# A hybrid decoder layer on one core: narrower scores, the softmax's 1/sum moved into the head's norm, a chained product, and two gates computed as a pair

## The chip, the cores and the metric

The kernel runs on one core of one Trainium2 chip. The metric is the device time of one execution in microseconds (us). Before the change the median of three runs is 1358.22 us (1357.28 to 1360.21).

The engines are named as in the profile: PE (TensorE, matmuls, with PEld for its weight loads), DVE (VectorE), ACT (ScalarE), POOL (GpSimd), and SP, whose queue issues most DMAs. Each engine works through its instructions in a fixed order, which is decided when the program is built, and waits at an instruction until what it needs is there.

## The reference

One layer on x of 1024 tokens by 1024 channels, all in float32:

```python
xn = rmsnorm(x, norm_mix_w)
da_q, da_k, da_v, sw_q, sw_k, sw_v, g_da, g_sw = split_cols(xn @ w_in)   # 4352 columns
y_da = diff_attention(da_q, da_k, da_v, lam, 0.2, subln_w)
y_sw = sliding_window_attention(sw_q, sw_k, sw_v, sinks)
merged = sigmoid(g_da) * (y_da @ w_br_da) + sigmoid(g_sw) * (y_sw @ w_br_sw)
x = x + merged @ w_mix_out
x = x + conv_ffn(rmsnorm(x, norm_ffn_w), ...)     # up, causal conv of width 3, silu(gate) * val, down
return rmsnorm(x, norm_final_w)
```

The differential attention has 4 heads. For each head two score matrices (c = 0, 1) are made from 64 channels each; both are causal, carry a linear bias, and go through a softmax:

```python
p = softmax(logits)                       # over all keys up to the query
a = p[:, :, 0] - lam * p[:, :, 1]
o = a @ v                                 # 128 channels a head
o = rmsnorm(o, subln_w) * (1.0 - lam_init)
```

The window attention has 8 query heads in 2 groups, a window of 128 keys, and a sink logit for each head that enters only the softmax's sum.

## The kernel before

Everything is kept transposed: channels on the 128 partitions, the 1024 tokens along the free axis (two halves of 512). A float32 operand is split into a high part (rounded to fp32r by ACT) and a low part (the rest, by a DVE subtraction), and a product is three matmuls: high by high, high by low, low by high. A plain projection of 128 output channels costs 24 matmuls of 512 columns for each half of the tokens.

`project` (L251 on) computes 34 blocks of 128 channels of `w_in`. Five are plain. Eight pairs of blocks go through a Strassen-Winograd scheme: each pair's 2 x 2 problem (two output blocks, two token halves) takes seven products of 12 matmuls (`product`, names P1 to P7) where the plain way takes eight. For that POOL forms four sums of the weights (`sum_pair`, L87), ACT and DVE split them (`split_pair`), and DVE puts the products together (`recombine`). The last 13 blocks, which are gates, are not computed there: they are kept as filler, 26 halves of 24 matmuls, and `HALVES` says behind which attention step each is placed (`back_half`). A query or key block that comes out of a pair is scaled on POOL, split, and stored twice by SP; a gate block is stored as it is.

`attention` runs six units: four differential heads, then the two groups of the window attention, eight steps of 128 queries each. In `da_step` (step i, w = (i + 1) * 128 keys) PE writes the scores of each c into `sc` (two matmuls for each chunk of up to 512 columns; the width is rounded up to a multiple of 256), DVE adds the bias and finds the row minimum (L570), ACT takes the exponential with its row sum (L571), DVE forms the reciprocal of the sum (L572). ACT then scales the second matrix by -lam/sum (L577), DVE scales the first by its 1/sum and adds (L578). PE transposes the result, ACT and DVE split it, and `da_av` multiplies it with v. `da_norm` takes the norm of the head, over 128 channels, from sums of squares (`col_sums`, `rstd_cols`) and applies it in two pieces, one and two steps later (`later`). `sw_step` does the same for four heads at once: L653 to L661 the softmax, L663 four divisions by the sum on DVE, L670 transposes, L680 products, L687 the result, which is stored to DRAM and read back (`rest`, L705) to be split for the branch projections.

`down` (L968 on) multiplies the hidden activations (22 blocks) with `w_dn`. Blocks 0 to 5 are plain: 16 pieces (m, c), m the output block, c the first or second three blocks of input; the banks `pss[m, hf]` hold m's sum until DVE adds it to the residual in `x3` (L1034). Blocks 6 to 13 go through the seven products again: a loop over four output pairs (L1037 on) makes A11 B11 into a bank `y` that is kept, and A12 B21 into a bank `ps`, and adds both to `x3` (L1044); then come the other five. The first pair's weight sums are made early ("sums" in `ahead`): its two raw tiles lie in the ring `raw`, which has three buffers and through which every weight load goes. PSUM has four banks `d` and four `y`.

Of the kernel before, what the change touches and what calls it, by code (L numbers as in the profile page):

```python
# [31 lines left out]
LPAD, RPAD = 480, 480  # L32
LAM_INIT = 0.2

HALVES = ((2,), (0, 0, 0, 0, 1, 1, 0, 0), (0, 0, 0, 0, 1, 0, 1, 1), (0, 0, 0, 0, 1, 0, 1, 1), (0, 0, 0, 1, 1, 0, 1, 0),
          (1, 0, 1, 1, 0, 1, 0, 0), (1, 0, 1, 1, 0, 1, 1, 0), (4,))
NEGMASK = 1e30


# [4 lines left out]
class Trunk:  # L44
# [23 lines left out]
    def ahead(self, n):  # L68
        while len(self.wq) < n and self.wsrc and (self.wsrc[0][1] != "pair" or self.uw):
            src, nk, *eng = self.wsrc.pop(0)  # L70
            if nk == "sums":

                self.sums = self.split_pair(*self.sum_pair(src, True), 1, 3)
# [12 lines left out]

    def sum_pair(self, src, first=False):  # L87
# [5 lines left out]
        v = self.tl(self.wp, [P, 2, 4, P], "raw", bufs=RAW) if first else self.tl(self.uw, [P, 2, 4, P], "rv", bufs=2)  # L93
# [3 lines left out]
        tt(sa[:, 0], v[:, 0], v[:, 1], ALU.add)  # L97
# [120 lines left out]
    def plan(self):  # L218

        self.kind = {m: "q" if m < 4 or 12 <= m < 16 else "k" if m < 8 or m == 16 else "v" if m < 18 else "g" for m in range(34)}  # L220


        self.plain = [0, 4, 8, 18, 20]
        self.pairs = [(1, 5), (9, 2), (6, 10), (3, 7), (11, 12), (13, 16), (17, 14), (15, 19)]
        gates = list(range(21, 34))
        self.back = []
        todo = [(m, hf) for m in gates for hf in range(2)]
        for steps in HALVES:
            self.back.append([[todo.pop(0) for _ in range(n)] for n in steps])
# [11 lines left out]
        self.pieces = [(m, c) for m0 in (0, 4) for c in range(2) for m in range(m0, m0 + 4)]  # L241
# [182 lines left out]
    def attention(self):  # L424
        nc, tc = self.nc, self.tc
        with ExitStack() as ctx:
# [27 lines left out]
            for u in range(6):  # L454
                if st is None:
                    st = self.q_stacks(u), self.kv_stacks(u)
                if u < 4:
                    self.v_parts(u)
                elif u == 4:
                    self.sw_v(self.v32(17))  # L460
                y = self.tl(self.fpool, [P, T], "y", bufs=2) if u < 4 else None
                aT = None
                for i in range(NB):
                    if u < 4:
                        if i % 2 == 0:
# [12 lines left out]
                if u < 4:  # L478
                    later = self.da_norm(u, y)
# [73 lines left out]
    def da_step(self, h, i, st, aT):  # L553
# [1 line left out]
        q, k = st  # L555
        slope = 4.0 ** -(h + 1)
        w = (i + 1) * P
        wp = (w + 255) // 256 * 256
        pr, rr = [], []
        for c in range(2):  # L560
            sc = self.tl(self.psS, [P, T], "sc")
            qs = q[c][:, i * P:(i + 1) * P]
            for part in range(2):
                for n0 in range(0, wp, H2):
                    n1 = min(n0 + H2, wp)
                    nc.tensor.matmul(sc[:, n0:n1], qs, k[c][part][:, n0:n1], start=part == 0, stop=part == 1)  # L566
# [3 lines left out]
            nc.vector.tensor_tensor_reduce(L[:, :w], sc[:, :w], self.bias[:, o:o + w], slope, 3e38, ALU.add, ALU.min, s[:, 0:1])  # L570
            nc.scalar.activation(L[:, :w], L[:, :w], AF.Exp, bias=s[:, 0:1], scale=-1.0, accum_out=s[:, 1:2])  # L571
            nc.vector.reciprocal(s[:, 2:3], s[:, 1:2])  # L572
            if c == 1:
                nc.vector.tensor_tensor(s[:, 2:3], s[:, 2:3], self.neglam, ALU.mult)
            pr.append(L)
            rr.append(s[:, 2:3])
        nc.scalar.mul(pr[1][:, :w], pr[1][:, :w], rr[1])  # L577
        nc.vector.scalar_tensor_tensor(pr[0][:, :w], pr[0][:, :w], rr[0], pr[1][:, :w], ALU.mult, ALU.add)  # L578
        qo = (i % 2) * P
        for j0 in range(0, i + 1, 4):  # L580
            nj = min(4, i + 1 - j0)
# [19 lines left out]
    def da_norm(self, h, y):  # L601

        nc, ap = self.nc, self.ap
        sqs = []
# [7 lines left out]

        def sums():
            self.col_sums(ssq, sqs[1:], 4, 4)
            box.append(self.rstd_cols(ssq, 8, P))

        def half(hf):
            ps = self.tl(self.psT, [P, H2], "t")
# [20 lines left out]
    def sw_step(self, g, n, st):  # L639
# [18 lines left out]
        for h in range(4):  # L658
            nc.scalar.activation(L[:, h, :w], L[:, h, :w], AF.Exp, bias=s[:, 0, h:h + 1], scale=-1.0, accum_out=s[:, 2, h:h + 1])
        nc.vector.tensor_tensor(s[:, 2, :], s[:, 2, :], s[:, 1, :], ALU.add)  # L660
        nc.vector.reciprocal(s[:, 3, :], s[:, 2, :])  # L661
        for h in range(4):
            self.last = nc.vector.tensor_scalar(L[:, h, :w], L[:, h, :w], s[:, 3, h:h + 1], None, ALU.mult)  # L663
        po = self.tl(self.psT, [P, H2], "t")
        nblk = w // P
        parts = []
# [301 lines left out]
    def down(self):  # L968

        nc, tc = self.nc, self.tc  # L970
        with ExitStack() as ctx:
# [31 lines left out]
            for i, (m, c) in enumerate(self.pieces):  # L1003
# [5 lines left out]
                for hf in range(2):  # L1009
# [3 lines left out]
                    for q, j in enumerate(js):  # L1013
                        h, l = self.hs[hf, j]
                        for p, (v, x) in enumerate(((w[0], h), (w[0], l), (w[1], h))):
                            nc.tensor.matmul(pss[m, hf], v[:, q, :], x, start=c == q == p == 0, stop=c == 1 and q == n - 1 and p == 2)
                if i in (2, 8):
                    ms = slice(i // 8 * 4, i // 8 * 4 + 4)
# [10 lines left out]
                if i == len(self.pieces) - 1:  # L1029
                    sums.pop(0)()  # L1030
                if c == 1:
                    for hf in range(2):
                        x = col(m, hf)
                        tt(x, x, pss[m, hf], ALU.add)  # L1034
# [168 lines left out]
```

## Time and profile before

| | |
|---|---|
| median of three runs | 1358.22 us |
| profiled execution | 1359.85 us, of which the span of the trace is 1358.0 us |
| mean granted clock of PE | 0.997 |
| projections | from the start to about 219.8 us |
| attention, first score to last window product | 240.2 to 495.8 us |
| branch projections, first | 509.2 us |
| plain pieces of the down-projection | 1112.2 to 1177.5 us |

In the views, a row of instructions gives start and duration in us, engine, line, operation and operands. A row of a window gives its length, then for PE, PEld, DVE, ACT and POOL the busy time and in brackets the number of instructions, then PE's granted clock (1.00 is full), the share of the DMA engines that were busy, and GB/s. A row of waits gives who waited for whom, the total, how often, and the longest. Matmuls overlap: one that takes 0.39 us starts 0.23 us behind the one ahead of it.

### The profile page before, as it was taken

The page shows a single profiled execution, that of the slowest core. Times are in us where ns is not written, and L with a number is a line of the kernel's source. Part 1 is how long each engine was busy: PE and PEld are TensorE (multiplying, and loading weights), DVE is VectorE, ACT ScalarE, POOL GpSimd, SP SyncE. Part 2 cuts the span into 40 slices and gives each one's busy share as a digit, 9 for nine tenths or more (in the row PEclk, how much of TensorE's full clock was granted, in tenths as well). Part 3 has the DMA queues.
Part 4 walks back from the last instruction along what each step waited for, and adds up shares of the span by engine and source line. Part 5 has one row for each costly group of instructions (what it writes and reads, how often), then busy time and mean ns, then how long its engine had stood idle before and what let it go on. Part 6 is the DMA issues. An engine that isn't in the chain of part 4 may idle for free.

```text
span 1358.0 us, 17192 instructions
## 1 busy us (share of the span) xinstructions
PE 1337.9 (99%) x6316; PEld 1106.8 (82%) x6316; DVE 1009.0 (74%) x1485; ACT 623.3 (46%) x975; POOL 464.7 (34%) x326
## 2 busy tenths in 40 slices
PE   8999999999999999999999999999999999999997
PEld 6888888788888888888878888888888888788886
DVE  8746774688778966445689889888988898886454
ACT  9432232678776764344354333433343344333343
POOL 0436641000000015642455565556555611231011
PEclk9999999999999999999999999999999999999999
DMA  6334436755654246324522222222222248551342
GB/s 255 140 110 164 145 140 219 205 150 144 171 134 146 79 129 228 140 95 131 162 78 94 78 78 93 69 87 78 93 66 89 85 157 303 190 180 70 92 133 86
DMA packets 62757, 179.50 MB, mean 132 GB/s; under 512 B 6864, under 2 KB 15184, under 8 KB 62672
## 3 DMA queue, kind: packets, MB, share of 16 engines
q1 hardware_dynamic: 50640, 159.93, 36.5%
q10 hardware_dynamic: 12032, 18.46, 3.7%
q8 instruction: 50, 0.82, 0.3%
q14 instruction: 35, 0.29, 0.1%
HBM read 129.61 MB, written 48.76 MB: 131 GB/s over the span
## 4 chain that ended last, share of the span: by engine, by line
PE 61%; DVE 19%; issue 9%; POOL 5%; DMA 2%; ACT 2%; POOLq 0%; SPq 0%; DVEq 0%; ACTq 0%
POOL us L958 5%; PE g L151 5%; PE g L153 5%; PE g L152 5%; PE t L828 4%; PE t L830 4%; PE t L829 4%; PE y L989 3%; PE d L989 3%; PE sc L153 3%; PE sc L152 3%; PE sc L151 3%; DVE wl L113 3%; DVE c L951 3%; PE sc L566 3%
## 5 line engine op out<-in xcount | busy, mean ns | idle before, releaser
L963 ACT ACTIVATE c<-us,vecs 128x1024 f32<-128x1024 f32 x44 | 54.8, 1248 | 163.1 <-POOL us L958 159.6
L958 POOL TENSOR_TENSOR us<-us,rstd 128x1024 f32<-128x1024 f32 x42 | 100.3, 2407 | 53.9 <-DVE wl L132 35.6
L130 ACT CAST wh<-raw 128x1024 fp32r<-128x1024 f32 (+2 forms) x62 | 62.8, 1012 | 110.2 <-PE sc L152 34.9
L111 ACT CAST sh<-sf 128x1024 fp32r<-128x1024 f32 x60 | 62.8, 1050 | 101.3 <-POOL sf L98 62.4
L132 DVE TENSOR_TENSOR wl<-raw,wh 128x1024 fp32r<-128x1024 f32 (+2 forms) x62 | 84.7, 1366 | 31.8 <-ACT wh L130 31.2
L964 DVE SCALAR_TENSOR_TENSOR c<-us,vecs,c 128x1024 f32<-128x1024 f32 x44 | 66.3, 1509 | 51.2 <-ACT c L963 51.2
L97 POOL TENSOR_TENSOR sf<-rv 128x512 f32<-128x512 f32 x29 | 41.9, 1446 | 162.0 <-DMA rv<-in_w_up 63.5
L113 DVE TENSOR_TENSOR sl<-sf,sh 128x1024 fp32r<-128x1024 f32 x60 | 83.7, 1397 | 8.0 <-ACT sh L111 8.0
L718 POOL TENSOR_TENSOR gr<-gr,rstd 128x1024 f32<-128x1024 f32 x16 | 40.3, 2521 | 130.3 <-PE t L670 91.1
L151 PE MATMUL g<-xh,wh 128*128 128x512 f32 x208 | 83.5, 402 | 0.3 <-ACT g L496 0.3
L152 PE MATMUL g<-xl,wh 128*128 128x512 f32 x208 | 83.1, 400 | 0.0
L153 PE MATMUL g<-xh,wl 128*128 128x512 f32 x208 | 82.8, 398 | 0.0
L168 POOL TENSOR_TENSOR rs<-ms,mhalf 128x8 f32<-128x8 f32 (+2 forms) x9 | 14.5, 1609 | 169.6 <-DVE ms L166 163.6
L570 DVE CUSTOM_DVE_ANT_0 L<-sc,bias 128x128 f32<-128x128 f32 (+7 forms) x64 | 47.9, 752 | 22.4 <-PE sc L566 17.3
L99 POOL TENSOR_TENSOR sf<-raw,rv 128x512 f32<-128x512 f32 x29 | 40.4, 1391 | 58.7 <-DVE sl L113 58.7
L965 DVE SCALAR_TENSOR_TENSOR c<-us,vecs,c 128x1024 f32<-128x1024 f32 x44 | 57.2, 1301 | 0.6
L98 POOL TENSOR_TENSOR sf<-sf,raw 128x512 f32<-128x512 f32 x30 | 56.7, 1890 | 1.6
L550 POOL MEMSET aT<- 128x128 f32 x32 | 6.1, 206 | 145.5 <-PE t L597 99.6
L113 DVE TENSOR_TENSOR wl<-raw,wh 128x1024 fp32r<-128x1024 f32 (+1 forms) x34 | 52.5, 1545 | 0.1
L566 PE MATMUL sc<-u,u 128*128 128x512 f32 (+1 forms) x192 | 51.1, 371 | 1.4 <-issue 0.8
L571 ACT ACTIVATE L<-L,sm 128x128 f32<-128x128 f32 (+7 forms) x64 | 49.4, 776 | 6.3 <-DVE sm L570 5.3
L151 PE MATMUL sc<-mh,wh 128*128 128x512 f32 x128 | 49.8, 389 | 0.0
(437 smaller groups left out, 4317.6 us busy)
## 6 DMA issues: line engine op xcount, KB each, us to landing
u<-qd SPq DMA_DIRECT2D x72, 256.0 KB, 6.6
raw<-in_w_down SPq DMA_DIRECT2D x28, 512.0 KB, 3.7
raw<-in_w_in SPq DMA_DIRECT2D x26, 512.0 KB, 4.2
hr<-hd SPq DMA_DIRECT2D x50, 256.0 KB, 5.3
raw<-in_w_up SPq DMA_DIRECT2D x23, 512.0 KB, 3.5
hd<-c SPq DMA_DIRECT2D x22, 512.0 KB, 2.7
rv<-in_w_up SPq DMA_DIRECT2D x21, 512.0 KB, 3.5
gr<-gd SPq DMA_DIRECT2D x16, 512.0 KB, 3.4
```

Source lines behind the costliest of these rows:

```text
L111: nc.scalar.copy(hi, src)
L113: nc.vector.tensor_tensor(lo, src, hi.bitcast(F32), ALU.subtract)
L130: self.hi = nc.scalar.copy(wh, raw)
L132: self.lo = (eng or nc.vector).tensor_tensor(wl, raw, wh.bitcast(F32), ALU.subtract)
L151: nc.tensor.matmul(ps, wh[:, kc + o, :], ah, start=first and n == 0, stop=False)
L152: nc.tensor.matmul(ps, wh[:, kc + o, :], al, start=False, stop=False)
L153: nc.tensor.matmul(ps, wl[:, kc + o, :], ah, start=False, stop=last and n == len(kcs) - 1)
L566: nc.tensor.matmul(sc[:, n0:n1], qs, k[c][part][:, n0:n1], start=part == 0, stop=part == 1)
L958: i = (nc.vector if m % NF == 0 else nc.gpsimd).tensor_tensor(us[:, 2:], us[:, 2:], self.rstd, ALU.mult)
L964: nc.vector.scalar_tensor_tensor(c, us[:, 1:T + 1], cw[1], c, ALU.mult, ALU.add)
L965: nc.vector.scalar_tensor_tensor(c, us[:, 0:T], cw[0], c, ALU.mult, ALU.add)
L989: nc.tensor.matmul(ps, v[:, n, :], x, start=n == i == 0, stop=n == len(js) - 1 and i == 2)
```

## The change

Six things are changed together.

1. `HALVES`, `pairs`: gates 21 and 22 become a ninth pair in the projections; 22 filler halves remain, placed anew.
2. `da_step`: the scores are computed for w columns only (i = 0 keeps 256). For w = 640 they are placed 128 columns into the tile, so that the chunks are 384 and 256 wide.
3. `da_step`, `da_norm`: the exponentials are no longer scaled by 1/sum. With s0 and s1 the two sums, the combination is p0 + p1 * (-lam * s0 / s1), which is s0 times the old one; s0 is kept for each query in a tile of the head, and the norm takes it out: the mean of squares is multiplied by 1/s0 squared, and the resulting factor by 1/s0, on POOL.
4. `sw_step`: the division of the fourth head goes from DVE to POOL; what the gates' first use waits for (`self.last`) becomes the reciprocal.
5. `down`: output blocks 4 to 7 come first in the pieces. For blocks 0 to 3 the first half's bank is not added to `x3` behind the pieces: A12 B21 is accumulated into it, and the sum is added once.
6. `sum_pair`: the second raw tile of the early sums lies in an `sl` buffer and not in the ring `raw`.

```diff
+        lo = P if w == 640 else 0
+        cuts = ((0, 256),) if i == 0 else ((0, w),) if w <= H2 else ((0, H2 - lo), (H2 - lo, w))
...
-                for n0 in range(0, wp, H2):
-                    n1 = min(n0 + H2, wp)
-                    nc.tensor.matmul(sc[:, n0:n1], qs, k[c][part][:, n0:n1], start=part == 0, stop=part == 1)
+                for n0, n1 in cuts:
+                    nc.tensor.matmul(sc[:, lo + n0:lo + n1], qs, k[c][part][:, n0:n1], start=part == 0, stop=part == 1)
...
-            nc.scalar.activation(L[:, :w], L[:, :w], AF.Exp, bias=s[:, 0:1], scale=-1.0, accum_out=s[:, 1:2])
-            nc.vector.reciprocal(s[:, 2:3], s[:, 1:2])
-            if c == 1:
-                nc.vector.tensor_tensor(s[:, 2:3], s[:, 2:3], self.neglam, ALU.mult)
+            nc.scalar.activation(L[:, :w], L[:, :w], AF.Exp, bias=s[:, 0:1], scale=-1.0, accum_out=s[:, 1:2] if c else self.s0[:, i:i + 1])
             pr.append(L)
-        nc.scalar.mul(pr[1][:, :w], pr[1][:, :w], rr[1])
-        nc.vector.scalar_tensor_tensor(pr[0][:, :w], pr[0][:, :w], rr[0], pr[1][:, :w], ALU.mult, ALU.add)
+        nc.vector.reciprocal(s[:, 2:3], s[:, 1:2])
+        nc.vector.tensor_scalar(s[:, 3:4], self.s0[:, i:i + 1], s[:, 2:3], self.neglam, ALU.mult, ALU.mult)
+        nc.vector.scalar_tensor_tensor(pr[0][:, :w], pr[1][:, :w], s[:, 3:4], pr[0][:, :w], ALU.mult, ALU.add)
...
-            box.append(self.rstd_cols(ssq, 8, P))
+            nc.vector.reciprocal(r0, s0)
+            nc.vector.tensor_tensor(t, r0, r0, ALU.mult)
+            nc.vector.tensor_tensor(t, t, ssq[:, :NB], ALU.mult)
+            rs = self.rstd_cols(t, 8, P)
+            nc.gpsimd.tensor_tensor(rs, rs, r0, ALU.mult)
...
-        nc.vector.reciprocal(s[:, 3, :], s[:, 2, :])
+        self.last = nc.vector.reciprocal(s[:, 3, :], s[:, 2, :])
         for h in range(4):
-            self.last = nc.vector.tensor_scalar(L[:, h, :w], L[:, h, :w], s[:, 3, h:h + 1], None, ALU.mult)
+            eng = nc.gpsimd if h in (3,) else nc.vector
+            eng.tensor_scalar(L[:, h, :w], L[:, h, :w], s[:, 3, h:h + 1], None, ALU.mult)
...
-        self.pairs = [(1, 5), (9, 2), (6, 10), (3, 7), (11, 12), (13, 16), (17, 14), (15, 19)]
-        gates = list(range(21, 34))
+        self.pairs = [(1, 5), (9, 2), (6, 10), (3, 7), (11, 12), (13, 16), (17, 14), (15, 19), (21, 22)]
+        gates = list(range(23, 34))
...
-                    for hf in range(2):
+                    for hf in range(m < 4, 2):
                         x = col(m, hf)
                         tt(x, x, pss[m, hf], ALU.add)
...
-                y, ps = bank(1), bank(0)
+                y, ps = bank(1), pss[m, 0]
...
-                self.product(ps, (wh[:, 4:8], wl[:, 4:8]), "B21")
+                self.product(ps, (wh[:, 4:8], wl[:, 4:8]), "B21", first=False)
```

`HALVES` (the lists are the units; the first entry stands ahead of them, the last behind them):

```diff
-HALVES = ((2,), (0, 0, 0, 0, 1, 1, 0, 0), (0, 0, 0, 0, 1, 0, 1, 1), (0, 0, 0, 0, 1, 0, 1, 1), (0, 0, 0, 1, 1, 0, 1, 0),
-          (1, 0, 1, 1, 0, 1, 0, 0), (1, 0, 1, 1, 0, 1, 1, 0), (4,))
+HALVES = ((2,), (0, 0, 0, 0, 1, 1, 0, 0), (0, 0, 0, 0, 1, 0, 0, 1), (0, 0, 0, 0, 1, 0, 1, 0), (0, 0, 0, 1, 1, 0, 1, 0), (1, 0, 0, 1, 0, 1, 1, 0), (1, 0, 1, 1, 0, 0, 1, 0), (3,))
```

More of the change, by code (lines that the diff above doesn't have):

```diff
@@ L71, in ahead @@
             if nk == "sums":
-                self.sums = self.split_pair(*self.sum_pair(src, True), 1, 3)
+                self.sums = self.split_pair(*self.sum_pair(src, True, "sl"), 1, 3)
             elif nk == "rest":
@@ L85, in ahead, with sum_pair @@
             self.wsrc[0] = src, nk, None, None, self.load_raw(src, nk)
-    def sum_pair(self, src, first=False):
+    def sum_pair(self, src, first=False, idle=None):
         nc = self.nc
@@ L92, in sum_pair @@
         nc.sync.dma_start(g.rearrange("p a k c -> p (a k) c"), src[0])
-        v = self.tl(self.wp, [P, 2, 4, P], "raw", bufs=RAW) if first else self.tl(self.uw, [P, 2, 4, P], "rv", bufs=2)
+        v = self.tl(self.wp, [P, 2, 4, P], "raw", bufs=RAW) if first and not idle else self.tl(self.uw, [P, 2, 4, P], idle or "rv", bufs=2)
         nc.sync.dma_start(v.rearrange("p a k c -> p (a k) c"), src[1])
@@ L240, in plan @@
         n, n2 = N1 // 2, NF - N1 - 8
-        self.pieces = [(m, c) for m0 in (0, 4) for c in range(2) for m in range(m0, m0 + 4)]
+        self.pieces = [(m, c) for m0 in (4, 0) for c in range(2) for m in range(m0, m0 + 4)]
         src += [(self.w_dn[m:m + 2, :, n * c:n * c + n, :].rearrange("m p k c -> p m k c"), 2 * n) for m, c in self.pieces[::2]]
@@ L464, in attention @@
                     if u < 4:
+                        if i == 0:
+                            self.s0 = self.tl(self.st, [P, NB], 's0', bufs=2)
                         if i % 2 == 0:
@@ L557, in da_step @@
         w = (i + 1) * P
-        wp = (w + 255) // 256 * 256
-        pr, rr = [], []
+        lo = P if w == 640 else 0
+        cuts = ((0, 256),) if i == 0 else ((0, w),) if w <= H2 else ((0, H2 - lo), (H2 - lo, w))
+        pr = []
         for c in range(2):
@@ L569, in da_step @@
             o = 896 - i * P
[L570 to L574 removed]
+            nc.vector.tensor_tensor_reduce(L[:, :w], sc[:, lo:lo + w], self.bias[:, o:o + w], slope, 3e38, ALU.add, ALU.min, s[:, 0:1])
+            nc.scalar.activation(L[:, :w], L[:, :w], AF.Exp, bias=s[:, 0:1], scale=-1.0, accum_out=s[:, 1:2] if c else self.s0[:, i:i + 1])
             pr.append(L)
[L576 to L578 removed]
+        nc.vector.reciprocal(s[:, 2:3], s[:, 1:2])
+        nc.vector.tensor_scalar(s[:, 3:4], self.s0[:, i:i + 1], s[:, 2:3], self.neglam, ALU.mult, ALU.mult)
+        nc.vector.scalar_tensor_tensor(pr[0][:, :w], pr[1][:, :w], s[:, 3:4], pr[0][:, :w], ALU.mult, ALU.add)
         qo = (i % 2) * P
@@ L603, in da_norm @@
         nc, ap = self.nc, self.ap
-        sqs = []
+        sqs, s0 = [], self.s0
         for hf in range(2):
@@ L614, in sums @@
             self.col_sums(ssq, sqs[1:], 4, 4)
-            box.append(self.rstd_cols(ssq, 8, P))
+            r0, t = (self.tl(self.st, [P, NB], n, bufs=2) for n in ("r0", "r2"))
+            nc.vector.reciprocal(r0, s0)
[3 more added lines that the diff above has]
+            nc.gpsimd.tensor_tensor(rs, rs, r0, ALU.mult)
+            box.append(rs)
         def half(hf):
@@ L1015, in down @@
                         for p, (v, x) in enumerate(((w[0], h), (w[0], l), (w[1], h))):
-                            nc.tensor.matmul(pss[m, hf], v[:, q, :], x, start=c == q == p == 0, stop=c == 1 and q == n - 1 and p == 2)
+                            nc.tensor.matmul(pss[m, hf], v[:, q, :], x, start=c == q == p == 0, stop=c == 1 and q == n - 1 and p == 2 and (m > 3 or hf > 0))
                 if i in (2, 8):
-                    ms = slice(i // 8 * 4, i // 8 * 4 + 4)
+                    ms = slice(4 - i // 8 * 4, 8 - i // 8 * 4)
                     nc.sync.dma_start(x3[:, ms], self.x2d[ms].rearrange("m p t -> p m t"))
```

## The prediction

> **What bounds the kernel now.** I read the page's busy times first, then PE's waits, then the timelines of the places that the change touches.
>
> ```profile
> PE 1337.9 (99%) x6316; PEld 1106.8 (82%) x6316; DVE 1009.0 (74%) x1485; ACT 623.3 (46%) x975; POOL 464.7 (34%) x326
> PE t L277 <- ACT wh L130: 6.6, 1, 6.6
> PE y L828 <- ACT wh L130: 1.1, 1, 1.1
> PE sc L566 <- issue: 0.8, 1, 0.8
> PE y L830 <- DVE wl L132: 0.6, 1, 0.6
> PE sc L566 <- DMA u<-qd: 0.6, 1, 0.6
> 219.77 0.39 PE L151 MATMUL g<-xh,wh 128*128 128x512 f32 x1
> 230.42 0.39 PE L153 MATMUL g<-xh,wl 128*128 128x512 f32 x1
> 309.40 0.28 PE L596 MATMUL t<-aT,v 128*128 128x256 f32 x1
> 311.43 0.28 PE L598 MATMUL t<-aT,v 128*128 128x256 f32 x1
> ```
>
> TensorE is the bound: 99% busy, and behind the 6.6 us of the first load its waits are a few tenths each. So time falls with matmuls that go, by the distance between two starts, not by the 0.39 us of one, since they overlap. From 219.77 to 230.42 lie the 48 matmuls of two gate halves: 10.65 / 47 = 0.2266 us for 512 columns. From 309.40 to 311.43 lie 18 of 256 columns: 2.03 / 17 = 0.119 us. What else can change is a wait, and the largest behind the start is this one:
>
> ```profile
> 1182.72 0.39 PE L830 MATMUL d<-h,wl 128*128 128x512 f32 x1
> 1184.23 0.50 PE L828 MATMUL y<-h,wh 128*128 128x512 f32 x1 [1.12 <-ACT wh L130]
> 1184.56 0.40 PE L829 MATMUL y<-h,wh 128*128 128x512 f32 x1
> 1185.57 0.50 PE L830 MATMUL y<-h,wl 128*128 128x512 f32 x1 [0.61 <-DVE wl L132]
> 1186.75 0.63 PE L828 MATMUL y<-h,wh 128*128 128x512 f32 x1
> 1187.18 0.63 PE L829 MATMUL y<-h,wh 128*128 128x512 f32 x1
> 1180.00:1200.00 20.00, 18.27 (x73) 14.33 (x72) 18.91 (x30) 8.90 (x14) 0.00 (x0) 0.91 0.65 215
> ```
>
> The second A12/A11 weight of the down-projection comes late: starts 1182.72 and 1184.23 are 1.51 apart instead of 0.23, 1184.56 and 1185.57 1.01, so 2.1 us are lost. Then the spacing is 0.43 instead of 0.23 for some eight matmuls, with the granted clock of the slice at 0.91: about 1.7 us more, 3.8 in all. [...]
>
> **The change, part by part.**
>
> *Ninth pair.* Gates 21 and 22 cost 4 halves of 24 matmuls; as a pair they cost 7 products of 12. 96 - 84 = 12 matmuls of 0.2266: **-2.7 us**. The pair adds POOL sums, splits and recombinations in the projections, where DVE has room beside PE:
>
> ```profile
> 180.00:200.00 20.00, 20.00 (x90) 16.57 (x89) 15.70 (x14) 6.42 (x8) 9.69 (x5) 1.00 0.34 132
> 271.50:306.60 35.10, 35.07 (x222) 30.27 (x222) 28.33 (x82) 27.51 (x62) 3.21 (x9) 1.00 0.56 157
> 402.25:495.80 93.55, 93.09 (x512) 76.96 (x511) 78.50 (x288) 64.20 (x188) 2.46 (x2) 1.00 0.34 109
> ```
>
> The first row is a pair: PE full, DVE 15.7 of 20. A ninth one of the same kind hides there. Its loads replace the two gates' loads; its two stores of `us` stand on SP where the last pair's three stood, ahead of the bias and the q/k stacks.
>
> ```profile
> 223.39 0.32 SPq L421 DMA_DIRECT2D qd<-us  x1
> 223.76 0.46 SPq L384 DMA_DIRECT2D gd<-us  x1
> 226.21 2.43 SPq L507 DMA_DIRECT2D u<-qd  x4
> ```
>
> Today the stacks follow at 226.21, 2.5 us behind the gate's store, which is ready at 223.76, itself held behind the key/query store at 223.39 (that one goes through POOL and ACT first). Two plain gate stores are ready about 1.5 us sooner, while by the order of the two programs 75 filler matmuls instead of 82 stand ahead of the first score (1.6 us less cover). This about cancels; the 0.8 us "issue" wait at that place may go: **-0.5** (-0.8 to +1.5).
>
> *Scores of used columns.* For i = 2, 4, 6 one chunk of 512 columns becomes 384: 3 steps x 2 c x 2 parts x 4 heads = 48 matmuls; no row shows 384 columns. Bounds: nothing saved (0), or as cheap as 256 (48 x 0.107 = 5.2). Between 0.119 and 0.2266 the middle is 0.173, since the spacing follows the columns at both ends: 48 x 0.054 = **-2.6**.
>
> *Sum in the norm.* Per step the ACT scaling and one reciprocal go; `tensor_tensor` on one column becomes `tensor_scalar`. Rows of the heads:
>
> ```profile
> L577 ACT ACTIVATE L<-L,sm 128x128 f32<-128x128 f32 (+7 forms) x32 | 24.3, 775 | 2.7 <-DVE sm L574 2.3 <-DVE sm L572 0.3
> L572 DVE RECIPROCAL sm<-sm 128x1 f32<-128x1 f32 x64 | 9.6, 157 | 6.2 <-ACT L L571 6.0
> ```
>
> ACT loses 24.3 us, DVE 32 x 0.157 = 5.0, and each chain from score to transpose is 0.8 us shorter. None of it is PE's time: worth 0 on its own; it is what pays for the lost filler. The norm gains a reciprocal, two products and one POOL product per head (about 0.16 each on DVE); its results are asked for a step later.
>
> *Lost filler.* In the attention PE has 4 of 26 gate halves (21.8 us) and 2.6 us of scores less to put over the DVE chains. A head (271.5 to 306.6) has DVE 28.3 of 35.1; it loses 1.3 us of DVE (8 x 0.157) and, by the order of the two programs, 1 to 4 us of PE, and stays between 80 and 86%. The window's part (402.25 to 495.80) is tighter: DVE 78.5, PE full in 93.6. In the program of the changed kernel 184 gate matmuls instead of 220 stand between the first and the last of its steps: 36 x 0.2266 = 8.2 us less, leaving 85.4 for DVE's 78.5 less one weight split (1.2) and the moved divisions:
>
> ```profile
> L663 DVE TENSOR_SCALAR L<-L,sw 128x256 f32<-128x256 f32 (+1 forms) x60 | 17.4, 344 | 0.3
> L653 DVE CUSTOM_DVE_ANT_0 L<-sc,bias 128x256 f32<-128x256 f32 (+1 forms) x52 | 19.8, 406 | 2.7 <-PE sc L650 2.7
> 198.98 2.41 POOL L386 TENSOR_TENSOR us<-us,rstd 128x1024 f32<-128x1024 f32 x1 [9.15 <-DVE us L402]
> 199.07 3.40 DVE L113 TENSOR_TENSOR sl<-sf,sh 128x1024 fp32r<-128x1024 f32 x1 [0.17 <-ACT sh L111]
> 1212.39 1.30 POOL L97 TENSOR_TENSOR c<-raw 128x512 f32<-128x512 f32 x1 [4.81 <-DVE sl L113]
> ```
>
> 60 divisions take 17.4, so 16 of them 4.6: DVE 72.7 of 85.4, 85% against 84% today. Stalls of PE grow little. Bounds: 0, and DVE's 72.7 with the 15.1 us of gaps that it has today (93.6 - 78.5), which is 87.8, 2.4 beyond 85.4, and as much again in the four heads: +5. Since a gap of DVE shrinks when its chain is asked for sooner, I take **+1.4**.
>
> *One of 4 divisions on GpSimd.* No row shows a POOL division. Bounds: 0.29 (DVE's pace) and 1.30 (POOL's sum of 512 columns, two inputs); I take half of that row, 0.65, less than the 0.9 that DVE's other three take beside it. POOL has 2.5 us of work in the window's 93.6. But a POOL operation can hold DVE: the split at 199.07 took 3.40 us, the whole 2.41 of POOL's operation longer than its usual 1.2. In a step, DVE's long operations read PSUM, and only the 4-column ones have two SBUF inputs, so I count 0 beyond the +1.4. [...]
>
> *End of attention.* The last window step's result is stored, read back and split; today
>
> ```profile
> 495.01 1.19 PE L680 MATMUL t<-aT,v 128*128 128x512 f32 x4
> 504.32 3.73 SPq L705 DMA_DIRECT2D yr<-yd  x4
> 512.91 2.36 DVE L749 TENSOR_TENSOR yl<-yr,yh 128x1024 fp32r<-128x1024 f32 x2 [0.21 <-ACT yh L748]
> ```
>
> 58 filler matmuls (13.1 us) and 24 of the first branch (5.4) cover it from 495.9 on, to 514.5; the last split ends at 515.3, used a little later. After the change 37 remain (8.4), but four of the next output's stand ahead and the halves interleave, so that the last part is used 18.8 us behind the last product instead of 20.5. Splits follow their loads, which wait for four buffers: **+0.4** (0 to +3).
>
> *Down-projection.* The chain into the first product's bank removes 4 of the 16 adds ahead of the stall, and holds `d` banks that nobody else needs. The `sl` buffer frees one of three raw buffers. The late weight is number two; ACT and DVE ahead of it:
>
> ```profile
> 1182.61 0.62 ACT L748 CAST h<-hr 128x512 fp32r<-128x512 f32 x1 [0.52 <-DVE hr L937]
> 1183.13 1.04 ACT L130 CAST wh<-raw 128x1024 fp32r<-128x1024 f32 x1
> 1176.56 1.21 DVE L132 TENSOR_TENSOR wl<-raw,wh 128x1024 fp32r<-128x1024 f32 x1
> 1183.70 0.68 DVE L1034 TENSOR_TENSOR x<-x,y 128x512 f32<-128x512 f32 x1
> 1184.30 1.21 DVE L132 TENSOR_TENSOR wl<-raw,wh 128x1024 fp32r<-128x1024 f32 x1
> ```
>
> Raw data is there; ACT's cast waits behind a cast that waits for DVE, and DVE has 11 operations of 0.6 between the first weight's split (1176.56) and the second's (1184.30). Four adds gone are 2.4 us. But the new order puts other splits into their place (12 operations between the two), and `sl` is loaded only when PE is done with the parts that lay there (eleven or twelve pieces in, about 1161), so POOL's sums and their splits move from about 1159 to 1165 and closer to the stall. Bounds: -3.8 (it goes) and +2 (as long again). I take **-1.5**, less than half of it. 3.8 - 1.5 = 2.3 would stay.
>
> **Sum**, against the profiled execution (span 1358.0, time 1359.85): -2.7 - 0.5 - 2.6 + 1.4 + 0.4 - 1.5 = -5.5, 1354.3. The median of the runs is 1358.22, 1.6 below the profiled one, so **1352.7 us**.
>
> **Rivals.** *The stall goes altogether and attention hides all:* -2.7 - 2.6 - 0.5 - 3.8 = -9.6, **1348.6**. For it: four adds fewer ahead of a 2.1 us delay; against: the order above. *The gain comes back as waits of PE in the attention*, +5 instead of +1.4: **1356.5**, no change. For it: DVE at 85% with chains; against: the window's steps run at 84% now with 0.5 us of PE idle. *Slower: GpSimd's quarter is late.* Place: the transposes of head 3 in each of 16 steps. If it takes 1.3 us and its start waits for DVE, a step's chain is 0.4 to 0.8 us longer and DVE is held 0.65; it decides from 85.4 us on, when a step exceeds 5.3 us of PE: 72.7 + 16 x 1.3 = 93.5, 8 us over. With half-clock stretches behind some gaps (1.7 each, two or three), 1352.7 + 8 + 4 = **1365**. For it: the row at 199.07; against: POOL is empty there.
>
> **How the numbers follow.** Forecast 60%, stall gone 16%, gain lost 12%, slower 12%. A measurement tells 0.2% (2.7 us) from nothing. Faster by that means below 1355.5: nearly all of the forecast (its own range 1350 to 1356) and the first rival, 74%; within 1355.5 to 1360.9: 14%; slower: 12%. The range 1348.5 to 1360 takes in the forecast and the first two rivals, and leaves the slower one out.
>
> **What would show it.** 6304 matmuls or so; 48 scores of 384 columns at 0.17 apart; the attention some 24 us shorter, projections 19 longer; PE's wait for `wh`/`wl` near 1180 between 0 and 2 us and the clock there 0.91 or 1.00; POOL divisions near 0.65. Wrong would make it: PE gaps over 1 us in the window's steps, DVE operations stretched beside POOL's divisions, or 384 columns paced like 512.

## The result, and the profile after

The changed kernel takes 1365.8 us (median of 6 runs, 1364.41 to 1366.56) against 1358.4 for the kernel before on the same chip: ratio 1.0054, 95% interval 1.0043 to 1.0066. It is slower by 7.4 us; 1352.7 was forecast, and the range ended at 1360. The span of its profiled execution is 1364.3 us.

The page of the changed kernel, busy times and granted clock by slices:

```profile
PE 1345.2 (99%) x6304; PEld 1104.3 (81%) x6304; DVE 1015.9 (74%) x1454; ACT 603.9 (44%) x942; POOL 485.5 (36%) x350
...
PEclk9999999999999999999999999999999999999999
```

The largest waits of PE (the 6.7 us of the first load left out; who waited for whom, total, how often, longest), and two windows, the steps of the window attention and the place of the old stall:

```profile
PE d L173 <- POOL rs L167: 1.0, 1, 1.0
PE d L158 <- ACT sl L1086: 0.8, 1, 0.8
PE sc L151 <- DVE yl L756: 0.7, 3, 0.3
PE g L150 <- DVE gr L741: 0.5, 1, 0.5
PE y L837 <- DVE wl L131: 0.5, 1, 0.5
PE t L687 <- DVE aT L681: 0.5, 2, 0.2
```

```profile
400.00:500.00 100.00, 98.18 (x552) 79.17 (x551) 85.80 (x315) 70.25 (x207) 17.56 (x18) 1.00 0.35 106
1180.00:1200.00 20.00, 19.53 (x86) 15.85 (x86) 19.68 (x29) 7.64 (x11) 0.00 (x0) 1.00 0.75 246
```

What was forecast of the work came: 6304 matmuls, 12 fewer; ACT 19.4 us less; and at 1180 the stall is down to one wait of 0.5 us, with 86 matmuls started in the slice instead of 73 and the clock at 1.00. The waits are small, too small for 7.4 us and the gain that was forecast besides; the two largest were there before, with 1.0 and 0.8 us. And PE is busy 7.3 us *more* than before (1337.9), with fewer matmuls at the same clock. So their starts must lie further apart. That shows where there is no wait. In the mix (384 matmuls of 512 columns), the first and the last before, then the first, the 49th and the last after:

```profile
596.22 0.39 PE L151 MATMUL sc<-mh,wh 128*128 128x512 f32 x1
683.03 0.39 PE L153 MATMUL sc<-mh,wl 128*128 128x512 f32 x1
```

```profile
598.58 0.40 PE L150 MATMUL sc<-mh,wh 128*128 128x512 f32 x1
610.33 0.39 PE L150 MATMUL sc<-mh,wh 128*128 128x512 f32 x1
687.00 0.39 PE L152 MATMUL sc<-mh,wl 128*128 128x512 f32 x1
```

Before, 86.81 / 383 = 0.2267 us from start to start. After, the first 48 hold two gaps: starts at 603.14 and 609.07 follow just behind the ends of DVE's operations on `ml`, at 603.09 and 609.01. From the 49th on there is none: 76.67 / 335 = 0.2289. In three products of the hidden layer (36 matmuls of the T operands with the sums of weights, `sh` and `sl`), before and after:

```profile
788.89 0.39 PE L828 MATMUL t<-T_0h,sh 128*128 128x512 f32 x1
796.82 0.39 PE L830 MATMUL t<-T_3h,sl 128*128 128x512 f32 x1
```

```profile
794.34 0.40 PE L835 MATMUL t<-T_0h,sh 128*128 128x512 f32 x1
802.47 0.39 PE L837 MATMUL t<-T_3h,sl 128*128 128x512 f32 x1
```

7.93 / 35 = 0.2266 became 8.13 / 35 = 0.2323. The diff touches neither stage. What the two stages share with it is memory: `s0`, `r0` and `r2` are new tiles of 32 bytes a partition, two buffers each, 192 bytes in the pool `st`, which lies ahead of the weights on the left side of SBUF. In the built programs the first raw weight tile lies at byte 9216 of a partition before, and at 9408 after; all later tiles of the left side move with it (`wh`, `wl`, the inputs of the branches and most of the hidden layer's). The right side (`xh`, `xl`, `mh`, `ml`, and in the hidden layer `sh`, `sl`) starts at the other end: `xh` is at 163328 in both programs. Before, the tiles of the large products all start at multiples of 512; after, left and right are 192 bytes out of step.

### The profile page after: what moved, and what is told of

The parts are those of the page before. It is cut to its first block, busy times and chain, and to the rows that moved or that the text cites. A ratio compares the mean times of both kernels' runs of the same rounds, so it can differ in the third digit from the quotient of the medians.

```text
span 1364.3 us, 17160 instructions
## 1 busy us (share of the span) xinstructions
PE 1345.2 (99%) x6304; PEld 1104.3 (81%) x6304; DVE 1015.9 (74%) x1454; ACT 603.9 (44%) x942; POOL 485.5 (36%) x350
## 4 chain that ended last, share of the span: by engine, by line
PE 86%; DVE 5%; POOL 3%; DMA 3%; issue 1%; ACT 1%; POOLq 0%; SPq 0%; ACTq 0%; DVEq 0%
PE t L837 14%; PE t L836 14%; PE t L835 14%; PE d L996 3%; PE y L996 3%; PE sc L568 3%; PE g L150 3%; PE g L151 3%; PE g L152 3%; DMA gr<-gd 2%; PE sc L152 2%; PE sc L150 2%; PE sc L151 2%; PE d L1023 2%; PE y L1023 2%; POOL gr L742 2%
## 5 line engine op out<-in xcount | busy, mean ns | idle before, releaser
L131 DVE TENSOR_TENSOR wl<-raw,wh 128x1024 fp32r<-128x1024 f32 (+2 forms) x60 | 75.8, 1263 | 41.5 <-ACT wh L129 31.6
L112 DVE TENSOR_TENSOR sl<-sf,sh 128x1024 fp32r<-128x1024 f32 x62 | 90.5, 1462 | 8.6 <-ACT sh L110 8.4
L150 PE MATMUL g<-xh,wh 128*128 128x512 f32 x176 | 70.6, 401 | 0.1
L152 PE MATMUL g<-xh,wl 128*128 128x512 f32 x176 | 70.5, 401 | 0.0
L151 PE MATMUL g<-xl,wh 128*128 128x512 f32 x176 | 70.3, 399 | 0.0
L152 PE MATMUL sc<-mh,wl 128*128 128x512 f32 x128 | 50.2, 392 | 0.0
```

Source lines behind the costliest of these rows:

```text
L112: nc.vector.tensor_tensor(lo, src, hi.bitcast(F32), ALU.subtract)
L131: self.lo = (eng or nc.vector).tensor_tensor(wl, raw, wh.bitcast(F32), ALU.subtract)
L150: nc.tensor.matmul(ps, wh[:, kc + o, :], ah, start=first and n == 0, stop=False)
L151: nc.tensor.matmul(ps, wh[:, kc + o, :], al, start=False, stop=False)
L152: nc.tensor.matmul(ps, wl[:, kc + o, :], ah, start=False, stop=last and n == len(kcs) - 1)
```

## The experiments

Each kernel is compared with the kernel before on the same chip; that one's median was 1356.7 to 1357.4 us in these series, so ratios are compared, and 0.1% is 1.36 us.

### Where the tiles lie

In the changed kernel, the left pad less 192 bytes:

```diff
-LPAD, RPAD = 480, 480
+LPAD, RPAD = 288, 480
```

> The changed kernel with the left pad at 288 bytes instead of 480. The change puts three new small tiles (3 x 2 buffers x 32 bytes = 192 bytes) into the pool that lies ahead of the weights on the left side of SBUF, so every later tile of that side lies 192 bytes further; 288 puts them back where the kernel before has them. Not one instruction differs. Theory 'placement': the distance between two 512-column matmuls goes from about 0.232 us back to 0.227 us in the projections, the mix and the hidden layer, some 8 us in all: about 1357.5 us (1356 to 1359). Rival 'work': the time was lost to what the change moved (filler, GpSimd's quarter of the divisions): unchanged, 1365 to 1367 us, with the spacing still 0.232.

Measured: 1354.8 us, ratio 0.9982 (0.9973 to 0.999). By the ratios (0.9982 against 1.0054) 9.8 us are back, where the theory gave some 8. The mix, and the same three products:

```profile
594.76 0.39 PE L150 MATMUL sc<-mh,wh 128*128 128x512 f32 x1
...
681.57 0.39 PE L152 MATMUL sc<-mh,wl 128*128 128x512 f32 x1
...
787.89 0.39 PE L835 MATMUL t<-T_0h,sh 128*128 128x512 f32 x1
...
795.82 0.39 PE L837 MATMUL t<-T_3h,sl 128*128 128x512 f32 x1
```

86.81 / 383 and 7.93 / 35: to the hundredth what they were before the change.

The other way round, in the changed kernel with `LPAD, RPAD = 480, 288`, and in the kernel before with `672, 480`:

> The changed kernel with the left side left as it is (192 bytes further) and the right pad at 288 instead of 480, which moves the tiles of the right side (the split inputs of the projections, the mix's inputs, the sums of weights) by the same 192 bytes. Placement theory, form 'distance': what counts is where the stationary tile lies relative to the moving one; both have moved alike, so the time is that of the left pad of 288, about 1357.5 us. Form 'own address': what counts is each tile's own address, in steps of 512 or 1024 bytes; now all tiles lie off, and it stays at 1365 us or gets slower, up to 1372. Rival 'work': 1365 to 1367.

> The kernel before with the left pad at 672 bytes instead of 480: its left tiles now lie where those of the changed kernel lie; no instruction differs from the kernel before. Placement: it loses what the changed kernel lost, 7 to 10 us: 1365 to 1368 us, with the spacing 0.232 instead of 0.227 in projections, mix and hidden layer. Rival 'work': 1358 us, within 0.1%.

Moving the right side along gives 1355.38 us, 0.9992 (0.9983 to 1.0001): the distance counts, not a tile's own place. The kernel before, with nothing but 192 bytes of pad added, takes 1366.34, 1.0066 (1.0053 to 1.0079): it becomes as slow as the changed one.

Which distances are good? The changed kernel with left pads of 32, 160 and 256, so with the left side 256, 128 and 32 bytes ahead of the old places:

> The changed kernel with the left pad at 32: all later tiles of the left side 256 bytes ahead of where the kernel before has them, the right side unmoved. Where the left and right tiles lie 0 or 512 bytes apart (counted modulo 512: 0) the spacing is 0.227; 192 bytes off it was 0.232. If only a multiple of 512 is good, 256 off costs as much as 192, 8 to 11 us: 1363 to 1366. If a multiple of 256 (or of 64 or 128 with 192 a bad case for another reason) does, it stays at 1354.8, within 1 us.

> The changed kernel with the left pad at 160: the left side 128 bytes ahead of the kernel before's places, the right side unmoved. 256 bytes off cost nothing, 192 off cost 11 us. If a multiple of 128 is enough: 1354.8, within 1 us. If only a multiple of 256 is good: 1360 to 1368, with spacings of 0.23 and above in the hidden layer.

> The changed kernel with the left pad at 256: the left side 32 bytes ahead of the kernel before's places, the right unmoved. 256 bytes off costs nothing, 192 costs 11 us, 128 15 us. If only multiples of 256 are good: 1362 to 1370. If the cost shrinks with the distance (32 is near to 0): 1355 to 1359.

| left side against right | us | ratio to before |
|---|---|---|
| in step (pad 288) | 1354.8 | 0.9982 |
| both sides 192 on | 1355.38 | 0.9992 |
| 192 on (as changed) | 1365.8 | 1.0054 |
| 32 ahead | 1370.02 | 1.0096 (1.0083 to 1.011) |
| 128 ahead | 1369.9 | 1.0093 (1.0079 to 1.0108) |
| 256 ahead | 1354.9 | 0.9982 (0.9973 to 0.999) |

0 and 256 are good, 32, 128 and 192 are bad, and 32 is no better than 128 (both came out at or just above the top of what was expected): a multiple of 256 bytes is what fits all six; other multiples of it were not tried. One more kernel sets the weights and the left side's other tiles apart. A pad of 64 bytes behind the weights' pool puts all later left tiles 256 bytes on and leaves `raw`, `wh` and `wl` at 192:

```diff
             self.wp = ctx.enter_context(tc.tile_pool(name="wp", bufs=2))
+            pad = ctx.enter_context(tc.tile_pool(name="pad_w", bufs=1))
+            pad.tile([P, 16], F32, name="pad_w_t")
```

> The changed kernel (left pad 480, so that the weights' tiles raw, wh and wl lie 192 bytes off as before this run) with a pad of 64 bytes put behind the weights' pool: all later tiles of the left side now lie 256 bytes off, which cost nothing when all of them did. Alone off are raw, wh and wl. If it is the pair of weight tile and input tile that counts, the projections, the filler and the mix keep 0.232 us (about 5 us of the loss) and the products of the hidden layer by the sums of weights (stationary sh, sl) go back to 0.227 (about 4 us): 1359.5 to 1362.5. If only the input tiles' places count: 1355. If only the places of raw, wh, wl count: 1364 to 1367.

Measured: 1358.85, 1.0012 (1.0002 to 1.0021), a little under the interval of the pair theory. The same two places of its timeline:

```profile
596.38 0.39 PE L150 MATMUL sc<-mh,wh 128*128 128x512 f32 x1
...
684.05 0.39 PE L152 MATMUL sc<-mh,wl 128*128 128x512 f32 x1
...
790.32 0.39 PE L837 MATMUL t<-T_0h,sh 128*128 128x512 f32 x1
...
798.26 0.39 PE L839 MATMUL t<-T_3h,sl 128*128 128x512 f32 x1
```

The products with `sh` and `sl`, whose two operands are in step again, are back at 7.94 / 35 = 0.2269. The mix, whose weights alone are off, stays as slow as in the changed kernel, at 87.67 / 383 = 0.2289. So it is the pair of stationary and moving operand of one product.

Products with both tiles on the left side show the same from the other side. Twelve matmuls of the down-projection take hidden activations `h` and weights `wh`, `wl` that all lie on the left. Their first and last, in the changed kernel, where both are 192 bytes on, and in this last kernel, where they are 256 and 192 on, so 64 apart:

```profile
1193.96 0.39 PE L835 MATMUL d<-h,wh 128*128 128x512 f32 x1
...
1196.45 0.39 PE L837 MATMUL d<-h,wl 128*128 128x512 f32 x1
```

```profile
1187.99 0.39 PE L837 MATMUL d<-h,wh 128*128 128x512 f32 x1
...
1190.51 0.39 PE L839 MATMUL d<-h,wl 128*128 128x512 f32 x1
```

Moved together they keep the old distance, 2.49 / 11 = 0.226 us; 64 bytes apart they take 2.52 / 11 = 0.229. In these rows the spacing of PE's own matmuls depends on how its two operands lie to each other, by 1 to 2.5%. What in the memory makes it so, the runs do not show.

### GpSimd's quarter of the divisions

The prediction's slower rival blamed it. Undone in the changed kernel as it is, then with the left pad at 288:

```diff
-            eng = nc.gpsimd if h in (3,) else nc.vector
+            eng = nc.gpsimd if h in () else nc.vector
```

> The changed kernel with all four divisions of a window step on VectorE again (only GpSimd's quarter undone). Rival of the prediction 'GpSimd's quarter is late': this undoes the loss, 1355 to 1360 us. Placement: the quarter is worth next to nothing, 1364 to 1368 us.

> The changed kernel with the left pad at 288 (places as in the kernel before) and all four divisions on VectorE. Theory 'the quarter moves nothing': 1354.1 to 1355.5, as with the tiles off, where undoing it gave 1363.5 against 1365.8. Rival 'VectorE is the bound in the window steps and GpSimd relieves it' (the prediction's sum leant on that: 72.7 of VectorE instead of 77.3 in 85.4): 1356 to 1359, with more waits of PE for VectorE between 400 and 500 us.

Measured: 1363.51, 1.0051 (1.0038 to 1.0063), and 1355.88, 0.9989 (0.9981 to 0.9998). Neither differs from its partner with the quarter (1.0054 and 0.9982) by more than the intervals: the rival falls, and so does a gain clear of noise. Why the gain is missing stands in the groups of the changed kernel on POOL and on DVE (busy time, mean ns), and of the same kernel with all 64 divisions on DVE:

```profile
L670 POOL TENSOR_SCALAR L<-L,sw 128x256 f32<-128x256 f32 (+1 forms) x16 | 15.7, 982 | 77.7 <-DVE sw L667 36.6 <-PE sc L656 10.1 <-DVE sw L661 8.9
```

```profile
L670 DVE TENSOR_SCALAR L<-L,sw 128x256 f32<-128x256 f32 (+1 forms) x48 | 18.2, 430 | 0.2
```

```profile
L670 DVE TENSOR_SCALAR L<-L,sw 128x256 f32<-128x256 f32 (+1 forms) x64 | 18.2, 340 | 0.2
```

16 divisions fewer, and DVE is busy with the other 48 as long as with 64: each became 0.09 us longer. One step of the changed kernel shows POOL beginning 0.15 us behind DVE and lying beside all three:

```profile
459.78 1.29 DVE L670 TENSOR_SCALAR L<-L,sw 128x256 f32<-128x256 f32 x3
459.93 0.99 POOL L670 TENSOR_SCALAR L<-L,sw 128x256 f32<-128x256 f32 x1 [6.73 <-DVE sw L667]
```

In the rows the 48 divisions are longer, 430 against 340 ns; three that began at 410.33, ahead of POOL's at 412.03, took 0.88 us together instead of the 1.29 at 459.78. The prediction counted 0 for this, since it took only operations with two SBUF inputs to be held, as the split at 199.07 was. For operations that read PSUM the kernel before bears it out: L403 at 106.84, inside POOL's operation from 105.83 to 109.18, took the same 0.68 us as L397 at 98.61, when POOL was idle. But a division has one SBUF tile as input and was held all the same. By what, no trace shows.

### The parts alone

Three parts of the change, each put alone into the kernel before (its places keep). The down-projection (hunks of `sum_pair`, `pieces` and `down`):

> The kernel before with the down-projection's part alone (pieces of the outputs 4 to 7 first, A12 B21 chained into the open bank, the second raw sum in the sl buffer); its tiles lie as in the kernel before. By the prediction's term: 1.5 us less than the kernel before, with 2.1 to 2.3 us of the stall near 1183 left. Rival: the stall of 2.1 us and its half-clock stretch is a matter of the one execution that was profiled, and most executions of the kernel before lose less there, so the part is worth 0 to 0.7 us by medians. Other rival: the stall goes altogether, 3.8 us less.

Measured: 1356.0, 0.9988 (0.998 to 0.9997), 1.6 us less. The window of the stall, in this kernel and then in the kernel before with the left pad of 672, which has none of this part:

```profile
1180.00:1200.00 20.00, 19.38 (x86) 15.73 (x85) 17.59 (x22) 9.82 (x15) 6.38 (x4) 1.00 0.53 168
```

```profile
1180.00:1200.00 20.00, 19.41 (x85) 15.33 (x84) 19.96 (x32) 7.70 (x11) 0.00 (x0) 1.00 0.66 215
```

The second row, at 1.00, shows that the lower clock (0.91 in the row of before) is not there in every execution of the old order; by medians the part is worth what was forecast.

The ninth pair with its filler table, and the scores of used columns:

> The kernel before with the ninth pair and the new filler table alone; tiles as in the kernel before. By the prediction's terms: -2.7 for 12 matmuls, -0.5 at the attention's start, and more than +1.4 for the filler since nothing is taken from VectorE here: 0 to 2 us less than the kernel before. Rival 'the gain comes back as waits in the attention': 0 to 3 us more, with waits of PE for VectorE between 400 and 500 us. Either way 19 us more of projections and as much less of attention.

> The kernel before with the scores of used columns alone (48 chunks of 384 columns in place of 512; the scaling on ScalarE and the sums stay). By the prediction's term 2.6 us less (0.054 us for each of 48). Rival: the heads are held by the chain through VectorE and ScalarE there, and the columns saved come back as waits of PE: within 0.7 us of the kernel before.

Both failed. The pair alone takes 1370.92, 1.0104 (1.0091 to 1.0117), 14 us more; the scores alone take 1361.61, 1.0031 (1.0019 to 1.0043), 4.2 us more. The window of 400 to 500 us for the kernel before, the pair, and the scores, and below it a window of the scores where a head passes into the window attention:

```profile
400.00:500.00 100.00, 99.54 (x545) 82.34 (x545) 80.86 (x297) 68.34 (x198) 4.37 (x3) 1.00 0.34 111
```

```profile
400.00:500.00 100.00, 93.83 (x542) 77.81 (x543) 86.55 (x330) 72.04 (x206) 1.84 (x2) 0.98 0.39 115
```

```profile
390.00:430.00 40.00, 36.03 (x224) 31.32 (x223) 35.45 (x133) 29.90 (x85) 1.68 (x1) 0.96 0.55 157
...
400.00:500.00 100.00, 97.29 (x539) 80.08 (x537) 81.73 (x307) 68.58 (x198) 4.07 (x2) 0.98 0.34 109
```

PE, idle for 0.5 us of the 100 before, is idle for 6.2 and 2.7 us, and the mean granted clock is 0.98. In the kernel with the scores alone 4 us of idle lie between 390 and 430. No filler was taken from it, and `HALVES` is the same; but the order in which the built program mixes filler and steps is another: 274 gate matmuls instead of 235 stand between the first score of the heads and the first of the window attention, and 211 instead of 249 from there to its last product. That the missing 38 make the idle time fits, but was not tested alone.

### The pair, its filler and the scores, with the rest in place

The changed kernel with the left pad at 288, without the pair (13 gates, old `HALVES`) and with all divisions on DVE; then the same with four of its 26 halves moved ahead of the first score, three from the attention's steps and one from behind its end:

> The changed kernel with the left pad at 288, without the ninth pair (13 gates and the old table of filler) and with all divisions on VectorE: scores of used columns, 1/sum in the norm and the down-projection's part stay. Theory 'the filler that the pair takes from the attention gives back what its 12 matmuls save': 1352.5 to 1354.5, as fast as or faster than with the pair. Rival (the prediction's terms, -2.7 for the pair against +1.4 for filler): 1355.5 to 1357, slower than with it.

```diff
-HALVES = ((2,), (0, 0, 0, 0, 1, 1, 0, 0), (0, 0, 0, 0, 1, 0, 1, 1), ...
+HALVES = ((6,), (0, 0, 0, 0, 1, 1, 0, 0), (0, 0, 0, 0, 1, 0, 0, 1), ...
```

> The kernel without the pair (1352.55 us) with four of its 26 filler halves taken out of the attention and put ahead of its first score, so that the attention and its end hold the same 22 halves less 2 as in the changed kernel; PE's work is the same to the matmul. Prediction's term for lost filler, +1.4: 1354 us. Theory now: the filler is worth what separates the kernels with and without the pair, 3.3 us plus the 2.7 that the pair saves, less 0.5 at the start: 5 to 6 us, so 1357.5 to 1358.5 us, with PE idle or half-clocked between 400 and 510 us. If it stays at 1352.5, the pair's loss is in its own work (sums, splits, stores) and not in the filler.

Without the pair: 1352.55 us, 0.9966 (0.9954 to 0.9979), the fastest of all, faster than both kernels. With the four halves ahead: 1361.92, 1.0035 (1.0022 to 1.0047), 9.4 us more, beyond the 5 to 6 expected, although PE has the same matmuls to do. The window of 400 to 500 us and the first matmul of the mix, without the pair and with the halves ahead, and the end of the attention in the latter:

```profile
400.00:500.00 100.00, 99.11 (x538) 81.92 (x537) 82.70 (x297) 70.57 (x199) 4.82 (x2) 1.00 0.36 113
...
593.07 0.39 PE L151 MATMUL sc<-mh,wh 128*128 128x512 f32 x1
```

```profile
400.00:500.00 100.00, 97.75 (x548) 80.39 (x548) 84.65 (x319) 69.00 (x202) 1.84 (x2) 0.99 0.37 109
...
480.00:520.00 40.00, 38.75 (x177) 30.71 (x176) 28.61 (x66) 26.79 (x55) 4.83 (x2) 0.96 0.50 166
...
599.49 0.39 PE L150 MATMUL sc<-mh,wh 128*128 128x512 f32 x1
```

The place of filler alone costs time: with less of it in the attention PE is idle for 2.25 us of the 100 instead of 0.89, and at the end for 1.25 of 40 at a clock of 0.96, while DVE has not reached 85 of 100, and the mix begins 6.4 us later. The phases from there on are 3 us longer too (spans of 1350.9 and 1360.1 us), in stretches of which nothing was changed; why, no run was made to tell.

From the kernel without the pair, the quarter given back to GpSimd, and the scores widened again:

> The kernel without the pair and with GpSimd's quarter of the divisions. With the pair the quarter was worth 1.0 us (1354.8 against 1355.9, intervals overlapping). Where PE has filler enough, VectorE is not waited for and the quarter is worth 0 to 0.7 us: 1351.8 to 1352.6. If it holds VectorE where it matters: 1353 or more.

> The kernel without the pair, with the scores as in the kernel before (whole multiples of 256 columns): the norm's and the down-projection's part are left. Prediction's term for the scores, -2.6 us: 1355.1. Rival: alone they made the kernel 4 us slower, since the order in the program moved with them, so their worth here may be nothing: 1352 to 1353.

The quarter makes it 1355.9, 0.9991 (0.9982 to 1.0): 3.4 us slower, the bad case. (Here the gates' first use also waits for the reciprocal and no longer for the last division, `self.last`.) But its mix begins here:

```profile
594.17 0.39 PE L151 MATMUL sc<-mh,wh 128*128 128x512 f32 x1
```

That is 1.1 us later than without the quarter, of 3.6 us between the two spans (1350.9 and 1354.5); the rest comes behind the mix, in the hidden layer and the down-projection, where the two programs are alike. That the quarter holds VectorE where it matters is therefore not shown. The wide scores make it 1358.24, 1.0015 (1.0006 to 1.0024), slower than either expectation. Here narrowing them is worth 6.7 us, where alone it cost 4.2. And the norm's part, which is what separates this kernel from the down-projection alone (0.9988), costs 3.7 us without the narrow scores; with them both gain 3.0 (0.9988 to 0.9966). Scores and norm cannot be priced singly.

## Why the prediction was wrong

The terms, each from two ratios (0.001 is 1.36 us; with their intervals each is known to about 2 us):

| | forecast, us | shown, us | by |
|---|---|---|---|
| scores and norm | -2.6 | -3.0 | 0.9988 to 0.9966 |
| down-projection | -1.5 | -1.6 | 1 to 0.9988 |
| pair, start, filler, quarter, end of attention | -1.4 | +2.2 | 0.9966 to 0.9982 |
| places of the tiles | not in the sum | +9.8 | 0.9982 to 1.0054 |
| sum | -5.5 | +7.4 | |

**The step that failed** is the first one, "time falls with matmuls that go, by the distance between two starts": it took 0.2266 us from the kernel before and let it stand for all 512-column matmuls of the changed one. That distance is not a property of the instruction alone: in the changed kernel it was 0.2289 in the mix and 0.2323 in the hidden layer. The part on the sum in the norm weighed the new operations and found them worth 0; it did not weigh the three new tiles. 192 bytes of them put every product with one operand on each side of SBUF out of step, 10 us. None of the rivals held this. The kernel's two pads of 480 bytes ahead of all pools, with the large products' tiles on multiples of 512 behind them, were there to be asked about.

**A size that was off:** the ninth pair, start, filler, quarter and end of attention together, -1.4. With the places restored they cost 2.2 us. Which of them was mis-sized stays open, since they cannot be priced singly either. The four kernels with and without pair and quarter:

| | without the quarter | with the quarter |
|---|---|---|
| without the pair | 0.9966 | 0.9991 |
| with the pair | 0.9989 | 0.9982 |

Without the quarter the pair (with its filler table) costs 3.1 us; beside the quarter it gains 1.2, close to the -1.4, though within the intervals. The quarter, counted as 0, costs 3.4 us without the pair and gains 1.0, within the intervals, with it. Filler can cost more than the bound of +5 named for it: moving four halves alone cost 9.4. The working compared DVE's sum with PE's (72.7 of 85.4) and took 85% as room. DVE's sum did not fall by the 4.6 us of moved divisions, since the other 48 became longer; and PE is idle for 6.2 us of the window in the pair's kernel and 2.25 with the halves ahead, with DVE at 86.55 and 84.65%. That a chain from score to product has to be covered step by step, not in sum, would explain it, but was not tested.

The working also took all 96 matmuls of the four halves from the attention, though by its own counts 7 of them stood ahead of the first score (82 to 75) and 21 behind the last product (58 to 37). The 68 that are left are 15.4 us, not 21.8. The attention, from first score to last product, became 14.7 us shorter (240.2 to 495.8 before, 259.2 to 500.1 after) where 24 were named; the 19 us longer projections came as named.

**Terms that held:** the down-projection (-1.6 for -1.5), with the wait at 1180 to 1190 at 0.5 us and the clock at 1.00, inside what was named. Scores and norm together (-3.0 for -2.6). The spacing that this term rests on came as well; one of the 384-column scores of the changed kernel and the next start:

```profile
340.05 0.34 PE L568 MATMUL sc<-u,u 128*128 128x384 f32 x1
340.22 0.60 PE L538 MATMUL t<-ident,f 128*128 128x128 f32 x4
```

They lie 0.17 us apart, as forecast. But matmul time saved was not kernel time saved: alone, the same 48 chunks cost 4.2 us, and each of the two parts was good only with the other, so that the sum came out near is in part luck.

**The slower rival** named 1365 us and would have been right by its number. Its mechanism was not: all divisions on DVE left the changed kernel at 1363.51. A division on POOL takes 0.98 us (0.65 was taken, 0.29 to 1.30 the bounds), and DVE's divisions beside it are stretched, which the prediction named as a sign of being wrong. But the loss lies in stages, such as the mix and the hidden layer, that have no division. The right number was luck.

With the places restored the changed kernel is at 0.9982, 2.4 us below before where 5.5 were forecast: the pair, its filler and the quarter are 3.6 short, the other two terms 0.5 over.

## What to carry to other kernels

Before a duration is carried from one program to another, look at what the change adds to memory: here 192 bytes in an early pool moved every later tile of the left side, and the spacing of untouched matmuls in a stage without waits showed it at once (0.2267 to 0.2289 us in the mix). Keep the moving and the stationary operands in step (here 0 and 256 bytes were good, and 32, 128 and 192 cost 9.8 to 15.5 us), and correct a pad when a small tile is added. Work that covers chains can have a worth beyond its own time: four halves cost 9.4 us here by their place alone. Price it by moving it alone, and expect parts that share a stage not to add.

## What was unexpected of the hardware

- The distance between the starts of two 512-column float32 matmuls depends on where stationary and moving tile lie to each other: 0.2267 us at 0 modulo 256 bytes, 0.2289 in the mix and 0.2323 in the hidden layer with the left side 192 bytes on, at an unchanged granted clock of 1.00. With 32 or 128 bytes it was no better: the whole kernel took 1370 us.
- A GpSimd division beside three on VectorE made each of those 0.09 us longer in the mean (340 to 430 ns), so 16 of 64 moved away saved VectorE nothing (18.2 us both ways).
